# Branch B's v projected 512 columns wide, half of the gate's pieces in attention's opening, and output banks in turn

## The chip, the core and the metric

The kernel runs on one core of a Trainium2 chip. The metric is the device time of one execution in microseconds, from runs of the kernel on the chip; a profiled execution gives the trace that is read here. TensorE (PE) multiplies matrices into PSUM, which has eight banks of 512 float32 columns; VectorE (DVE) and ScalarE (ACT) read PSUM; GpSimd (POOL) works on SBUF alone; the queue of SyncE (SP) issues all DMA transfers, in the order of the program.

## What is computed

One layer on x, 1024 positions of 1024 channels, in float32. It has two parallel attention branches of eight heads each, and everything starts from one modulated, normalised input h:

```
ada = c @ w_ada + b_ada;  shift, scale, gate = split(ada, 3)
h = rms_norm(x, norm_w) * (1 + scale) + shift
cq(384), ckv(256), k_rope(32), gate_a(512), q_b(512), k_b(512), v_b(512), f_b(8),
    gate_b(512), mg_a(1024), mg_b(1024) = split(h @ w_in)
A: latent attention from cq and ckv with rotary parts; B: q_b, k_b normalised, forget-gate bias
y_a = o_a * silu(gate_a);  y_b = o_b * silu(gate_b)
merged = sigmoid(mg_a) * (y_a @ w_branch_a) + sigmoid(mg_b) * (y_b @ w_branch_b)
out = x + gate * (merged @ w_out)
```

The change touches v_b (512 columns of w_in for branch B's v), the `gate` vector of 1024 numbers (c times a third of w_ada, plus a bias) and the last product.

## The kernel before, in words

Every product is made in three matmuls: each operand is split into a rounded high part and the low rest (`split`: ACT copies the high part, DVE subtracts), and hi x hi, hi x lo and lo x hi are summed in one bank. All instructions are issued in the order of the Python program; each engine keeps its own order and waits on semaphores.

The stages. `phase0` makes h, transposed, as hT_hi and hT_lo. `latents`, `g2q` (4 steps) and `g2k` (4 steps, L771) make branch A's q, k and v and store them in DRAM. `attention` (L1239) runs the 16 heads, eight of A and then eight of B, each in 12 steps of scores, softmax, transposes and products. `output` (L1299) makes the last product in 16 units of 24 matmuls.

Between these, a generator of filler work, `fillers` (L909), is advanced by `fill_to` (L142) until a planned TensorE time is reached; a matmul of n columns counts n / 2.4 + 2 ns there. The filler begins with `g1b` (L805), the projection of branch B's q, k and v. It works on six chunks of 256 columns of weights (ci 0 and 1 for q, 2 and 3 for k, 4 and 5 for v). A chunk has four units, each of two blocks of 128 positions in one bank; a unit is 48 matmuls and pauses after every six, which makes eight pieces a unit and 192 pieces in all. The next chunk's weights (two loads of 512 KB) are requested in a chunk's first unit and split in its second and third. A v unit is evacuated by ACT and DVE into `vhl` and stored one unit later (`store_b`, L875). When q, k and v are done, `fillers` goes on with the units named f: the gates, the merge gates and, at the end, the two branches' projections, whose loads of the first weight are started by `hook` from inside g1b.

The accumulators of the filler alternate over the bank tags in `self.fbanks` (`fbank`, L905): "fo" until q, k and v are done, then "fg", and "fgott" after attention. `output` took its banks in its own order, "ttof".

The gate vector is made on DVE: eight pieces, each a load of 512 KB (`gate_load`, L881) and one multiplication with a sum (`gate_sum`, L885). Before, pieces 0 to 3 are summed within g2k's first two steps and 4 to 7 at the beginning of attention; `gate_row` (L894), at head 3, step 0, adds the bias and transposes the column on TensorE (pgT). In attention's opening (L1247 to L1268) the first pair's q and k are loaded (qs, ks) and transposed (qt, kt) in five steps, and then seven score blocks of head 0 follow, each with 1500 ns of filler.

Of the kernel before, what the change touches and what calls it, by code (L numbers as in the profile page):

```python
# [10 lines left out]
F32 = mybir.dt.float32  # L11
F32R = mybir.dt.float32r
# [7 lines left out]
P = 128  # L20
S = 1024
D = 1024
KT = 8
# [51 lines left out]
class Net:  # L75
# [729 lines left out]
    def g1b(self, hook):  # L805
# [4 lines left out]
        def load(ci):  # L810
            if ci < 6:
                w[ci] = [self.load_w(t["w_b"][ci, :, 4 * e:4 * e + 4], [P, 4, 256], f"b{ci}_{e}") for e in range(2)]
# [5 lines left out]
        for ci in range(6):  # L818
            kind, half = ci // 2, ci % 2
            for sp in range(4):  # L820
                if sp == 0:
                    load(ci + 1)
                if sp in (1, 2) and ci < 5:
                    w[ci + 1][sp - 1] = self.split(w[ci + 1][sp - 1], f"b{ci + 1}_{sp - 1}")
                if ci == 5 and sp in (0, 2):
                    hook()
                acc = self.fbank(f"b{ci}_{sp}")
                for i in range(2):
                    st = 2 * sp + i
                    sl = slice(st * P, (st + 1) * P)  # L830
                    for kt in range(KT):
                        wh, wl = w[ci][kt // 4]
                        for e, (a, b) in enumerate(((self.hT_hi, wh), (self.hT_hi, wl), (self.hT_lo, wh))):
                            self.mm(acc[:, i * 256:(i + 1) * 256], a[:, kt, sl], b[:, kt % 4],
                                    kt == 0 and e == 0, kt == KT - 1 and e == 2)
                            if e == 2 and kt % 2 and (i, kt) != (1, KT - 1):
                                yield False
                a3 = acc.rearrange("p (g d) -> p g d", d=64)
                if kind == 2:
                    vhl = U.get([P, 8, P], F32R, f"bv{ci}_{sp}")  # L840
                    nc.scalar.copy(vhl[:, :, 0:64], a3)
                    nc.vector.tensor_tensor(out=vhl[:, :, 64:128], in0=a3, in1=vhl[:, :, 0:64].bitcast(F32), op=ALU.subtract)
                    self.store_b((self.vb_d[2 * sp:2 * sp + 2, :, half * 4:half * 4 + 4].rearrange("s p h d -> p s h d"),
                                  vhl.bitcast(F32).rearrange("p (s h) d -> p s h d", s=2), (U, vhl)))
                else:
                    o = Hs.get([P, 8, 64], F32, f"bo{ci}_{sp}")
                    sq = Hs.get([P, 8, 64], F32, f"bsq{ci}_{sp}")
                    nc.scalar.copy(o, a3)
                    nc.scalar.activation(sq, o, AF.Square)
                    if sp == 0:  # L850
                        ssq = self.sp.tile([P, 32], F32, tag="bssq", bufs=2, name=f"bssq{ci}")
                        outs = []
                    nc.vector.reduce_sum(ssq[:, 8 * sp:8 * sp + 8], sq, axis=AX.X)
                    Hs.put(sq)
                    self.store_b()
                    outs.append(o)
                    if sp == 3:
                        r = self.rsqrt(ssq, 32, 64, f"b{ci}_{sp}")
                        dst = (self.qb_d, self.kb_d)[kind]
                        items = []  # L860
                        for j, o in enumerate(outs):
                            nc.vector.tensor_tensor(out=o, in0=o, op=ALU.mult,
                                                    in1=r[:, 8 * j:8 * j + 8].unsqueeze(2).broadcast_to([P, 8, 64]))
                            items.append((dst[2 * j:2 * j + 2, :, half * 256:half * 256 + 256].rearrange("s p c -> p s c"),
                                          o.rearrange("p (s h) d -> p s (h d)", s=2), (Hs, o)))
                        self.store_b(*items)
                if sp == 3:
                    for pair in w.pop(ci):
                        U.put(*pair)
                if (ci, sp) == (5, 3):  # L870
                    self.store_b()
                    self.g1b_done = True
                yield 1000.0

# [19 lines left out]
    def gate_row(self):  # L894

        nc = self.nc
        nc.vector.tensor_tensor(out=self.gcol, in0=self.gcol, in1=self.b_gate, op=ALU.add)
# [341 lines left out]
    def attention(self):  # L1239
        N = len(self.seq)  # L1240
# [58 lines left out]
    def output(self):  # L1299
# [12 lines left out]
        for u in range(2 * ST):  # L1312
# [21 lines left out]
    def build(self):  # L1334
# [36 lines left out]
        with tc.manual_schedule():  # L1371
            with tc.tile_pool(name="ps2a", bufs=1, space=PSUM) as self.ps2:
# [26 lines left out]
                for sp in range(4):  # L1399
# [3 lines left out]
                    if sp < 3:  # L1403
# [22 lines left out]
def layout(i):  # L1426
# [39 lines left out]
    o["w_b"] = np.stack([_chunks(w_in[:, 1184 + 256 * c:1184 + 256 * (c + 1)], 8) for c in range(6)])  # L1466
# [28 lines left out]
```

## Time and profile before

| | |
|---|---|
| timed runs, median of 3 | 973.12 us (972.27 to 975.09) |
| the profiled execution | 970.98 us |
| its span, first to last instruction | 969.0 us |
| mean granted TensorE clock | 0.998 of 2.4 GHz |
| TensorE busy, share of the span | 98% |
| DVE, ACT, POOL busy | 66%, 49%, 21% |
| filler's q, k, v matmuls (b) | 88.7 to 285.4 us |
| DMA moved | 124.99 MB, mean 129 GB/s |

The busy share of TensorE is that of a pipelined engine: the durations of neighbouring matmuls overlap, so the time that a matmul costs is the distance from one start to the next. Idle time of another engine costs nothing by itself. The granted clock is shown as a share of 2.4 GHz; a row that shows less than 1.00 has a part at 1.2 GHz.

### The profile page before, as it was taken

The page shows a single profiled execution, that of the slowest core. Times are in us where ns is not written, and L with a number is a line of the kernel's source. Part 1 is how long each engine was busy: PE and PEld are TensorE (multiplying, and loading weights), DVE is VectorE, ACT ScalarE, POOL GpSimd, SP SyncE. Part 2 cuts the span into 40 slices and gives each one's busy share as a digit, 9 for nine tenths or more (in the row PEclk, how much of TensorE's full clock was granted, in tenths as well). Part 3 has the DMA queues.
Part 4 walks back from the last instruction along what each step waited for, and adds up shares of the span by engine and source line. Part 5 has one row for each costly group of instructions (what it writes and reads, how often), then busy time and mean ns, then how long its engine had stood idle before and what let it go on. Part 6 is the DMA issues. An engine that isn't in the chain of part 4 may idle for free.

```text
span 969.0 us, 15332 instructions
## 1 busy us (share of the span) xinstructions
PE 952.2 (98%) x5582; PEld 832.3 (86%) x5582; DVE 636.0 (66%) x1379; ACT 477.6 (49%) x959; POOL 204.0 (21%) x260
## 2 busy tenths in 40 slices
PE   7999999999999999999999999999999999999998
PEld 7999999999988888788888888888888878887887
DVE  3967977787646667567667676677676766596222
ACT  7776634443245656546555566465655644143000
POOL 0022132200011222122233233232332220045000
PEclk9999999999999999999999999999999999999999
DMA  9821132864943224225232232322411554633321
GB/s 348 322 95 45 50 116 81 295 225 169 312 134 98 87 67 131 66 74 155 79 109 67 66 90 67 114 85 88 132 56 44 185 185 153 245 141 125 109 88 66
DMA packets 80987, 124.99 MB, mean 129 GB/s; under 512 B 5928, under 2 KB 47536, under 8 KB 80912
## 3 DMA queue, kind: packets, MB, share of 16 engines
q1 hardware_dynamic: 80912, 124.01, 39.3%
q8 instruction: 44, 0.72, 0.3%
q14 instruction: 31, 0.25, 0.1%
HBM read 88.33 MB, written 35.66 MB: 128 GB/s over the span
## 4 chain that ended last, share of the span: by engine, by line
PE 89%; DVE 4%; DMA 3%; ACT 2%; issue 2%; POOL 0%; SPq 0%; ACTq 0%; DVEq 0%
PE f L127 31%; PE b L127 12%; PE out L127 9%; PE s L127 9%; PE o L127 7%; PE pt L136 6%; PE q L127 3%; PE ckv L127 2%; PE kv L127 2%; PE cq_s L127 2%; DVE hT_lo L998 1%; DMA ks_u<-ka_d 1%; PE cq_t L127 1%; DVE mg_h L991 1%; PE pada L127 1%
## 5 line engine op out<-in xcount | busy, mean ns | idle before, releaser
L1192 ACT CAST pp_u<-pt 128x512 fp32r<-128x512 f32 x192 | 92.2, 480 | 178.9 <-PE pt L136 164.9
L1193 DVE TENSOR_TENSOR pp_u<-pt,pp_u 128x512 fp32r<-128x512 f32 x192 | 106.5, 555 | 76.5 <-ACT pp_u L1192 74.4
L127 PE MATMUL f<-hT_hi,hi_f_u 128*128 128x512 f32 x384 | 153.9, 401 | 0.0
L127 PE MATMUL f<-hT_lo,hi_f_u 128*128 128x512 f32 x384 | 153.7, 400 | 0.0
L127 PE MATMUL f<-hT_hi,lo_f_u 128*128 128x512 f32 x384 | 153.5, 400 | 0.0
L127 PE MATMUL s<-k_u,q_u 96*128 96x512 f32 (+6 forms) x480 | 117.1, 363 | 1.2 <-ACT p_h L1172 0.7
L127 PE MATMUL b<-hi_b_u,hT_hi 128*128 128x256 f32 x384 | 109.6, 286 | 0.0
L127 PE MATMUL b<-hi_b_u,hT_lo 128*128 128x256 f32 x384 | 108.6, 283 | 0.0
L127 PE MATMUL b<-lo_b_u,hT_hi 128*128 128x256 f32 x384 | 108.6, 283 | 0.0
L1176 POOL TENSOR_SCALAR p_u<-p_u,rs 128x640 f32<-128x640 f32 (+1 forms) x64 | 64.7, 1011 | 169.1 <-DVE rs L1175 93.2
L1166 DVE TENSOR_REDUCE nm<-s 128x1 f32<-128x128 f32 (+7 forms) x128 | 97.0, 758 | 4.4
L127 PE MATMUL o<-pp_u,v_u 128*128 128x512 f32 (+7 forms) x384 | 94.4, 340 | 0.0
L1176 POOL TENSOR_SCALAR p_h<-p_h,rs 128x128 f32<-128x128 f32 (+1 forms) x64 | 36.9, 577 | 249.3 <-DVE rs L1175 220.0
L127 PEld LDWEIGHTS s<-k_u,q_u 96*128 96x128 f32 (+2 forms) x480 | 77.1, 191 | 7.0 <-ACT p_h L1172 1.2
L127 PEld LDWEIGHTS f<-hT_hi,lo_f_u 128*128 128x128 f32 x384 | 72.5, 189 | 12.0
L127 PEld LDWEIGHTS f<-hT_hi,hi_f_u 128*128 128x128 f32 x384 | 72.7, 189 | 11.1
L127 PEld LDWEIGHTS f<-hT_lo,hi_f_u 128*128 128x128 f32 x384 | 72.5, 189 | 11.2
L127 PEld LDWEIGHTS o<-pp_u,v_u 128*128 128x128 f32 (+1 forms) x384 | 62.0, 162 | 19.7 <-issue 0.2
L127 PEld LDWEIGHTS b<-lo_b_u,hT_hi 128*128 128x128 f32 x384 | 73.6, 192 | 0.3
L127 PEld LDWEIGHTS b<-hi_b_u,hT_hi 128*128 128x128 f32 x384 | 73.6, 192 | 0.3
L127 PEld LDWEIGHTS b<-hi_b_u,hT_lo 128*128 128x128 f32 x384 | 73.6, 192 | 0.0
L136 PEld LDWEIGHTS pt<-ident,p_u 128*128 128x128 f32 x416 | 52.7, 140 | 16.7
(310 smaller groups left out, 1998.5 us busy)
## 6 DMA issues: line engine op xcount, KB each, us to landing
raw_f_u<-in_w_t SPq DMA_DIRECT2D x24, 512.0 KB
wada_u<-in_w_ada SPq DMA_DIRECT2D x16, 512.0 KB
mg_d<-th_h SPq DMA_DIRECT2D x32, 256.0 KB
mg_h<-mg_d SPq DMA_DIRECT2D x32, 256.0 KB
raw_b_u<-in_w_b SPq DMA_DIRECT2D x12, 512.0 KB
x_u<-in_x SPq DMA_DIRECT2D x8, 512.0 KB
raw_wg_u<-in_w_gate SPq DMA_DIRECT2D x8, 512.0 KB
va_d<-vhl_u SPq DMA_DIRECT2D x8, 512.0 KB
```

The costliest lines, as they stand in the source:

```text
L127: self.nc.tensor.matmul(out, lhsT=l, rhs=r, start=start, stop=stop)
L136: self.nc.tensor.transpose(out=out, in_=in_, identity=self.ident)
L991: nc.vector.scalar_tensor_tensor(out=m, in0=m, scalar=1.0, in1=acc, op0=ALU.add, op1=ALU.mult)
L998: nc.vector.tensor_tensor(out=self.hT_lo[x], in0=mA[c1][:, x[2]], in1=self.hT_hi[x].bitcast(F32), op=ALU.subtract)
L1166: nc.vector.tensor_reduce(out=nm, in_=sv, axis=AX.X, op=ALU.max, negate=True)
L1176: nc.gpsimd.tensor_scalar(out=p[:, 0:w], in0=p[:, 0:w], scalar1=rs, scalar2=0.0, op0=ALU.mult, op1=ALU.add)
L1192: nc.scalar.copy(ph[:, c0:], pt[:, c0:])
L1193: nc.vector.tensor_tensor(out=pl[:, c0:], in0=pt[:, c0:], in1=ph[:, c0:].bitcast(F32), op=ALU.subtract)
```

## The change

1. g1b's chunks 4 and 5 become one v part. Its weights come as four loads of two of the eight row blocks each, all 512 columns wide (bv_0 to bv_3), requested in k's last chunk (ci 3). They are split in that chunk: bv_0 and bv_1 in its second and third unit, as before for a next chunk, bv_2 at the start of its fourth unit, and bv_3 in the middle of that unit, when the first half of chunk 3's weights has been given back. v then has eight units of 24 matmuls of 512 columns, one block of 128 positions each, with a pause after every three. `hook` is called before the second and the sixth of them; before, it was called before units 1 and 3 of chunk 5.
2. Gate pieces 4 to 7 are no longer loaded in g2k but in the opening of attention: 4 and 5 after the third of its five first steps, 6 and 7 after the fifth, where 4 and 5 are summed; 6 and 7 are summed before the sixth score block, where the bias is added too. It was added in `gate_row` before.
3. `output` takes its accumulators from `fbank`, in turn over "fgott".

```diff
--- before.py
+++ after.py
@@ -808,22 +808,22 @@
         def load(ci):
-            if ci < 6:
+            if ci == 4:
+                w[4] = [self.load_w(t["w_bv"][:, 2 * e:2 * e + 2], [P, 2, 512], f"bv_{e}") for e in range(4)]
+            elif ci < 4:
                 w[ci] = [self.load_w(t["w_b"][ci, :, 4 * e:4 * e + 4], [P, 4, 256], f"b{ci}_{e}") for e in range(2)]
...
-        for ci in range(6):
+        for ci in range(4):
             kind, half = ci // 2, ci % 2
             for sp in range(4):
                 if sp == 0:
                     load(ci + 1)
-                if sp in (1, 2) and ci < 5:
+                if sp in (1, 2) or (ci, sp) == (3, 3):
                     w[ci + 1][sp - 1] = self.split(w[ci + 1][sp - 1], f"b{ci + 1}_{sp - 1}")
-                if ci == 5 and sp in (0, 2):
-                    hook()
@@ -833,44 +833,60 @@
...
                             self.mm(acc[:, i * 256:(i + 1) * 256], a[:, kt, sl], b[:, kt % 4],
                                     kt == 0 and e == 0, kt == KT - 1 and e == 2)
+                            if (ci, sp, i, kt, e) == (3, 3, 1, 3, 2):
+                                U.put(*w[3][0])
+                                w[4][3] = self.split(w[4][3], "b4_3")
                             if e == 2 and kt % 2 and (i, kt) != (1, KT - 1):
                                 yield False
...
-                if kind == 2:
-                    vhl = U.get([P, 8, P], F32R, f"bv{ci}_{sp}")
-                    nc.scalar.copy(vhl[:, :, 0:64], a3)
-                    nc.vector.tensor_tensor(out=vhl[:, :, 64:128], in0=a3, in1=vhl[:, :, 0:64].bitcast(F32), op=ALU.subtract)
-                    self.store_b((self.vb_d[2 * sp:2 * sp + 2, :, half * 4:half * 4 + 4].rearrange("s p h d -> p s h d"),
-                                  vhl.bitcast(F32).rearrange("p (s h) d -> p s h d", s=2), (U, vhl)))
-                else:
...
+                if sp == 3:
+                    for pair in w.pop(ci)[ci // 3:]:
                         U.put(*pair)
-                if (ci, sp) == (5, 3):
-                    self.store_b()
-                    self.g1b_done = True
                 yield 1000.0
+        w = w[4]
+        for st in range(ST):
+            if st in (1, 5):
+                hook()
+            acc = self.fbank(f"bv_{st}")
+            sl = slice(st * P, (st + 1) * P)
+            for kt in range(KT):
+                wh, wl = w[kt // 2]
+                for e, (a, b) in enumerate(((self.hT_hi, wh), (self.hT_hi, wl), (self.hT_lo, wh))):
+                    self.mm(acc, a[:, kt, sl], b[:, kt % 2], kt == 0 and e == 0, kt == KT - 1 and e == 2)
+                if st == ST - 1 and kt % 2:
+                    U.put(*w[kt // 2])
+                if kt < KT - 1:
+                    yield False
+            a3 = acc.rearrange("p (g d) -> p g d", d=64)
+            vhl = U.get([P, 8, P], F32R, f"bvhl_{st}")
+            nc.scalar.copy(vhl[:, :, 0:64], a3)
+            nc.vector.tensor_tensor(out=vhl[:, :, 64:128], in0=a3, in1=vhl[:, :, 0:64].bitcast(F32), op=ALU.subtract)
+            self.store_b((self.vb_d[st], vhl.bitcast(F32), (U, vhl)))
+            if st == ST - 1:
+                self.store_b()
+                self.g1b_done = True
+            yield 1000.0
@@ -894,7 +910,6 @@
-        nc.vector.tensor_tensor(out=self.gcol, in0=self.gcol, in1=self.b_gate, op=ALU.add)
         pg = self.bank("t", "pgT")
@@ -1247,14 +1262,21 @@
         next(preps[0])
         self.fill_to(self.pe_time + 10000)
         self.load_v(0)
-        self.gate_sum(range(4, 8))
-        self.U.put(self.cb)
-        for _ in range(5):
+        for i in range(5):
             next(preps[0])
             self.fill_to(self.pe_time + 1500)
+            if i == 2:
+                self.gate_load((4, 5))
+            if i == 4:
+                self.gate_sum((4, 5))
+                self.gate_load((6, 7))
         for c, i in enumerate((0, 4, 1, 5, 2, 3, 6)):
             if c == 3:
                 self.load_v(1)
+            if c == 5:
+                self.gate_sum((6, 7))
+                self.U.put(self.cb)
+                nc.vector.tensor_tensor(out=self.gcol, in0=self.gcol, in1=self.b_gate, op=ALU.add)
@@ -1321,7 +1343,7 @@
-                acc = self.bank("ttof"[(u + e) % 4], f"out{u}{e}")[:, ls]
+                acc = self.fbank(f"out{u}{e}")[:, ls]
@@ -1400,7 +1422,7 @@
                     self.g2k(sp)
                     if sp < 2:
                         self.gate_sum((2 * sp, 2 * sp + 1))
-                    if sp < 3:
+                    if sp < 1:
                         self.gate_load((2 * sp + 2, 2 * sp + 3))
                     self.fill_to(self.pe_time + 6500)
@@ -1463,7 +1485,8 @@
-    o["w_b"] = np.stack([_chunks(w_in[:, 1184 + 256 * c:1184 + 256 * (c + 1)], 8) for c in range(6)])
+    o["w_b"] = np.stack([_chunks(w_in[:, 1184 + 256 * c:1184 + 256 * (c + 1)], 8) for c in range(4)])
+    o["w_bv"] = _chunks(w_in[:, 2208:2720], 8)
```

The rest of the diff moves q's and k's evacuation, which is unchanged, one level to the left.

## Rows read from the trace of the kernel before

**Rows 1.** Page, parts 1, 2 (GB/s in 40 slices of 24.2 us) and 5.
```profile
PE 952.2 (98%) x5582; PEld 832.3 (86%) x5582; DVE 636.0 (66%) x1379; ACT 477.6 (49%) x959; POOL 204.0 (21%) x260
...
GB/s 348 322 95 45 50 116 81 295 225 169 312 134 98 87 67 131 66 74 155 79 109 67 66 90 67 114 85 88 132 56 44 185 185 153 245 141 125 109 88 66
...
L127 PE MATMUL b<-hi_b_u,hT_hi 128*128 128x256 f32 x384 | 109.6, 286 | 0.0
```

**Rows 2.** Waits of TensorE, whole span: who <- for whom: us, times, longest.
```profile
PE pgT L136 <- DVE gcol L897: 2.4, 1, 2.4
PE out L127 <- DVE mg_h L991: 1.7, 1, 1.7
PE kt L136 <- DMA ks_u<-ka_d: 1.6, 1, 1.6
PE s L127 <- ACT p_h L1172: 0.7, 1, 0.7
```

**Rows 3.** Chain of waits, pieces in order of time: start us, us, what.
```profile
217.56 2.75 PE kv L127 x12
...
225.92 7.19 PE b L127 x60
...
258.81 10.16 DMA ks_u<-ka_d
...
815.76 16.66 PE f L127 x73
```

**Rows 4.** Timeline around pgT, DVE and PE: start us, us, instruction [idle before <-releaser].
```profile
391.07 0.29 DVE L1193 TENSOR_TENSOR pp_u<-pt,pp_u 128x128 fp32r<-128x128 f32 x1
...
393.83 0.16 DVE L1175 RECIPROCAL rs<-sm 128x1 f32<-128x1 f32 x1 [0.64 <-ACT p_u L1172]
393.91 0.15 DVE L897 TENSOR_TENSOR gcol<-gcol,vec 128x8 f32<-128x8 f32 x1
394.11 0.27 PE L136 MATMUL pgT<-ident,gcol 128*8 128x128 f32 x1 [2.40 <-DVE gcol L897]
```

**Rows 5.** Windows after pgT: us, busy PE PEld DVE ACT POOL, granted clock, DMA, GB/s.
```profile
394.10:395.30 1.20, 1.19 (x6) 1.01 (x7) 0.28 (x1) 0.00 (x0) 1.03 (x1) 1.00 0.00 0
...
395.30:398.80 3.50, 3.50 (x13) 2.76 (x12) 0.68 (x1) 1.64 (x3) 0.00 (x0) 0.53 0.83 202
```

**Rows 6.** Timeline, PE and DVE, from the last f to the first output.
```profile
875.54 0.39 PE L127 MATMUL f<-yhi_u,lo_f_u 128*128 128x512 f32 x1
...
876.87 0.68 DVE L991 SCALAR_TENSOR_TENSOR mg_h<-mg_h,f 128x512 f32<-128x512 f32 x1
...
877.60 0.50 PE L127 MATMUL out<-hi_wo_u,hT_hi 128*128 128x512 f32 x1 [1.68 <-DVE mg_h L991]
...
880.12 1.46 DVE L998 TENSOR_TENSOR hT_lo<-mA_u,hT_hi 128x512 fp32r<-128x512 f32 x2
```

**Rows 7.** Timeline in g2k, DVE and the SP queue.
```profile
231.45 1.29 DVE L800 TENSOR_TENSOR kraw_h<-kraw_h,y_g2k 128x512 f32<-128x512 f32 x2
...
236.63 2.16 SPq L877 DMA_DIRECT2D kb_d<-bo_h  x4
```

**Rows 8.** Tiles raw_b_u and raw_wg_u: count, ns min/median/max, first and last start.
```profile
L116 DVE TENSOR_TENSOR lo_b_u<-raw_b_u,hi_b_u x24: 675/682/1224, 85.7 to 249.4; 128x512 fp32r<-128x512 f32 x24
...
L890 DVE SCALAR_TENSOR_TENSOR raw_wg_u<-raw_wg_u,cb_u x8: 1212/1219/1221, 204.3 to 261.3; 128x1024 f32<-128x1024 f32 x8
```

**Rows 9.** Timeline of attention's opening, SP, PE and DVE.
```profile
259.58 4.34 SPq L1047 DMA_DIRECT2D k_u<-kr_d  x4
...
269.11 0.63 PE L136 MATMUL kt<-ident,ks_u 128*128 128x128 f32 x4 [1.58 <-DMA ks_u<-ka_d]
...
274.31 0.45 PE L127 MATMUL s<-k_u,q_u 96*128 96x128 f32 x3
...
289.71 0.11 DVE L1164 MEMSET s<- 64x64 f32 x1 [1.87 <-PE s L127]
...
294.64 0.33 PE L136 MATMUL pt<-ident,p_h 128*128 128x128 f32 x1 [0.32 <-POOL p_h L1176]
```

**Rows 10.** Waits of the SP queue, 183 to 300 us: us, times, longest.
```profile
SPq L877 <- DVE bv_u L842: 17.9, 5, 8.3
```

More of the change, by code (lines that the diff above doesn't have):

```diff
@@ L838, in g1b @@
                 a3 = acc.rearrange("p (g d) -> p g d", d=64)
-                if kind == 2:
-                    vhl = U.get([P, 8, P], F32R, f"bv{ci}_{sp}")
-                    nc.scalar.copy(vhl[:, :, 0:64], a3)
-                    nc.vector.tensor_tensor(out=vhl[:, :, 64:128], in0=a3, in1=vhl[:, :, 0:64].bitcast(F32), op=ALU.subtract)
-                    self.store_b((self.vb_d[2 * sp:2 * sp + 2, :, half * 4:half * 4 + 4].rearrange("s p h d -> p s h d"),
-                                  vhl.bitcast(F32).rearrange("p (s h) d -> p s h d", s=2), (U, vhl)))
-                else:
[L846 to L854, printed above, removed]
-                    self.store_b()
[L856 to L866, printed above, removed]
@@ L867, in g1b @@
-                if sp == 3:
-                    for pair in w.pop(ci):
+                o = Hs.get([P, 8, 64], F32, f"bo{ci}_{sp}")
+                sq = Hs.get([P, 8, 64], F32, f"bsq{ci}_{sp}")
+                nc.scalar.copy(o, a3)
+                nc.scalar.activation(sq, o, AF.Square)
+                if sp == 0:
+                    ssq = self.sp.tile([P, 32], F32, tag="bssq", bufs=2, name=f"bssq{ci}")
+                    outs = []
+                nc.vector.reduce_sum(ssq[:, 8 * sp:8 * sp + 8], sq, axis=AX.X)
@@ new lines, in g1b @@
+                Hs.put(sq)
+                self.store_b()
+                outs.append(o)
+                if sp == 3:
+                    r = self.rsqrt(ssq, 32, 64, f"b{ci}_{sp}")
+                    dst = (self.qb_d, self.kb_d)[kind]
+                    items = []
+                    for j, o in enumerate(outs):
+                        nc.vector.tensor_tensor(out=o, in0=o, op=ALU.mult,
+                                                in1=r[:, 8 * j:8 * j + 8].unsqueeze(2).broadcast_to([P, 8, 64]))
+                        items.append((dst[2 * j:2 * j + 2, :, half * 256:half * 256 + 256].rearrange("s p c -> p s c"),
+                                      o.rearrange("p (s h) d -> p s (h d)", s=2), (Hs, o)))
+                    self.store_b(*items)
@@ L869, in g1b @@
+                if sp == 3:
+                    for pair in w.pop(ci)[ci // 3:]:
                         U.put(*pair)
-                if (ci, sp) == (5, 3):
-                    self.store_b()
-                    self.g1b_done = True
                 yield 1000.0
+        w = w[4]
[18 more added lines that the diff above has]
+            if st == ST - 1:
+                self.store_b()
+                self.g1b_done = True
+            yield 1000.0
@@ L1239, in attention @@
     def attention(self):
-        N = len(self.seq)
+        nc, N = self.nc, len(self.seq)
         preps = {n: self.prep_a(n) if n < 8 else self.prep_b(n) for n in range(0, N, 2)}
```

## Prediction

> **What bounds the kernel now.** I read the engine shares first: TensorE is busy 952.2 of 969.0 us, DVE two thirds and ACT half [rows 1]. So a microsecond comes from fewer or shorter matmuls, or from a place where TensorE stands. Second, TensorE's waits over the whole span: besides the start there are four of note, pgT 2.4, out 1.7, kt 1.6 and s 0.7 us [rows 2], and the change touches the code at all four. Third, the chain of waits for the spacing of the matmuls, because a matmul's own duration (286 ns in the groups [rows 1]) overlaps its neighbours'. Last, timelines around each wait, to see what is late next. The reader should see that hardly any cover is left: whatever delays TensorE is added to the end. The profiled execution took 970.98 us (969.0 of span, 2.0 around it); I make the sum against it, and add 2.1 at the end, because the median of the timed runs is 973.12.
>
> **v at 512 columns.** Branch B has 3 x 384 matmuls of 256 columns in six weight chunks [rows 1]; v has two of the six, so 384. They become 192 of 512. Spacing: 60 matmuls of 256 in 7.19 us are 119.8 ns; 73 of 512 in 16.66 us are 228.2 ns; 12 of kv in 2.75 us, just after the narrow ones, 229.2 ns [rows 3]. So 46.0 us become 43.8: **-2.2 us** (-2.0 by kv's rows). The reason is a fixed part of about 11 ns in each matmul (2 x 119.8 - 228.2), paid half as often. The evacuations stay eight of 128x512 on ACT and DVE, the eight stores stay 512 KB each.
>
> The Trainium skill speaks against this term: its page TensorE: Matmul & The Clock Gate, section "Wait — 56ns, not 53.3ns?", gives a warm matmul's spacing as columns over 2.4 GHz plus about 2.5 ns. By that, as an estimate, 109.2 and 215.8 ns, the term would be -0.5 us and the whole change -5.1. The rows above do not agree with so small a fixed part.
>
> **The gate bias, added early.** At (3, 0) TensorE reaches pgT and stands 2.40 us, because the addition to gcol is queued on DVE behind a reciprocal that itself waits 0.64 us for ACT's sum [rows 4]. The change makes the addition in the opening, over 100 us earlier. pgT then needs its "t" bank alone, whose last reader starts at 391.07 and takes 0.29 us [rows 4], before TensorE stops at 391.7. There is more: the granted clock was 0.53 over the 3.5 us from 395.3 on, against 1.00 just before [rows 5]: nearly all of it at 1.2 GHz instead of 2.4. That cost 0.47 x 3.5 = 1.65 us of work, and the only idle stretch ahead of it is this one. Both go: **-4.1 us**. At worst something else holds TensorE as long: 0.
>
> **Output banks in turn.** The first output takes the "t" bank that the last unit but one of branch B's projection filled, and DVE is behind there: TensorE waits 1.68 us for its mg_h (876.87, 0.68 us) [rows 6]. In turn over five banks it takes the bank filled four units earlier, long free. Next is the last operand: hT_lo's final two pieces start at 880.12, 1.46 us for both [rows 6], so the first, which the first output needs in its last matmul, is there at about 880.8. From 875.77 that matmul, 23 spacings of 228 ns later, comes at 881.0. A tie: **-1.7 us**, at worst 0.
>
> **v's weights split early.** In the order of issue k's last chunk ends in piece 128 of 192 (a piece is six narrow matmuls or three wide ones, 652 and 646 ns in the planner's account), three pieces into the fill after the third g2k. Two v splits move from v's units into k's last unit. The last is issued behind that g2k's own DVE work, which ends with two products from 231.45, 1.29 us [rows 7]. A split's two differences take 0.68 us each [rows 8], 0.6 apart like those two products, so its first half is ready at about 233.4. The first v unit starts at 225.92 + 18 x 0.12 = 228.1 [rows 3] and wants that half in its 20th matmul, 19 x 0.228 later, at 232.4. TensorE stands: **+1.0 us** (0 to 1.6). On ACT the split's copies lie ahead of one evacuation, which has the idle TensorE time after it. The split it replaces, two units later, hid behind narrow matmuls, so nothing is earned there. Its 1.3 us on DVE also delay the normalised k, for whose store the SP queue waits until 236.63 [rows 7], and behind that store stand all stores and loads of attention's opening.
>
> **The opening: loads.** ks lands 10.16 us after its issue [rows 3], and the first kt transposes wait 1.58 us for it [rows 9]. Ahead of it lie the same bytes as before (the first f weight load now ahead of the stores instead of among them), so it lands about 1 us later (1.3 from the queue's start, less what the earlier f load fills). TensorE gets there 1.0 later by the stall above, 0.5 earlier by the shorter pieces (48 of 0.685 against 46 of 0.72). **+0.3 us** (-1.6 if ks is in time, +1.0).
>
> Four of eight gate loads move here. The first two (1.05 MB) are put between ks and the four loads of k's rotary rows, and behind a v store that waits for its evacuation. At 312 GB/s of this stretch [rows 1] they are 3.4 us on the queue. Before, those four issues began at 259.58 and the scores that read them started at 274.31 [rows 9]; no view names their landing. If they trail ks by one store and two gate loads, some 5 us, they meet the scores, which are also 5 us behind ks (274.31 - 269.11). I take **0**, with 0 to +3; a price below 0 is excluded, for a later issue cannot help.
>
> **The opening: DVE.** A gate piece is 1.22 us [rows 8]. Four stood ahead of q's products, where TensorE did not wait. Now two stand ahead of the first row maximum: the scores need that bank again only two steps later, some 5 us, so nothing. Two more and the bias stand ahead of the maximum of (0, 3). DVE is idle 1.87 us just before it [rows 9] and the sums take 2.4; the transposes after it already wait 0.32 us for POOL [rows 9], so **+0.6 us** (0 to 2.4). The s wait of 0.7 [rows 2] came from the last v evacuation on DVE between two score steps; that is now one step earlier: **-0.7** (0 at worst).
>
> Hooks and store order shift nothing else on TensorE: f's count and its order of banks stay, four of its matmuls just begin a step earlier.
>
> **Sum.** -2.2 - 4.1 - 1.7 + 1.0 + 0.3 + 0 + 0.6 - 0.7 = -6.8, so 964.2 for a profiled execution, and 966.3 for the median of timed runs.
>
> **Rivals** (all on the timed scale).
> 1. The opening gets worse: ks or k's rotary rows land so late that TensorE stands 2 to 3 us more and, as after pgT's 2.40, falls to 1.2 GHz for 1.65. For it: 1.6 us are late already, and the queue starts later. Against it: waits of 1.58 and 1.68 us left the clock at 1.00. -6.8 + 2.5 + 1.65 = -2.7: 970.4. Chance 0.18.
> 2. pgT's wait is only handed on: the reciprocal and ACT's sum are as late as before, and the next transposes or scores wait for them, with the clock drop. For it: TensorE arrives 2.4 us earlier at everything after. Against it: the next scores come some 3 us of f matmuls later, and the other even heads show no wait at this place [rows 2]. -6.8 + 4.1 = -2.7: 970.4. Chance 0.10.
> 3. The wide matmuls gain nothing, by a smaller fixed part than the rows show, or by v pieces that alternate with transposes: -6.8 + 2.2: 968.5. Chance 0.07. The page above would make nearly this.
> 4. All gains and no new wait, ks in time: -2.2 - 4.1 - 1.7 - 0.7 - 1.6 = -10.3: 962.8. Chance 0.15.
> 5. Slower: the SP queue, in order, stands at a v store for as long as it did once before, 8.3 us [rows 10], now with two gate loads and k's rotary rows behind it instead of ahead. The scores then wait about 8.3, plus 1.65 at 1.2 GHz: -6.8 + 10 = +3.2: 976.3. It decides from the point where those rows land more than 7 us after the scores are due. Against it: the store they now follow is of a unit that ends in TensorE's order well ahead. Chance 0.04.
>
> **Numbers.** The forecast, 964 to 968.5, has 0.46. The predicted time is 966.3. The range 962.0 to 970.6 leaves out rival 5 and the tails of 1, 2 and 4. A measurement of this kernel tells about 0.3%, 2.9 us, from no change: faster is below 970.2. The forecast, rivals 3 and 4 and some four tenths of 1 and 2 make faster 0.79; most of the rest of 1 and 2 makes the same 0.16; slower 0.05.
>
> **What would show it.** In the changed kernel's rows: b at 256 columns 768 and v 192 matmuls of 512 at 227 to 232 ns; no wait at pgT and no stretch below 1.00 at 395 us; the first out directly behind the last f; a wait of about 1 us in the first v unit on lo_b; kt waiting about 2 us. A wait of over 2 us in 228 to 295 us with a clock below 1.00 would make the prediction wrong upward; a kt that does not wait, downward.

## The result, and the profile after

The changed kernel takes 962.75 us (median of four runs, 961.75 to 964.47) against 973.12 for the kernel before, run beside it: ratio 0.9892, 95% interval 0.9865 to 0.9918, so 1.1% faster. A fourth execution of the kernel before, at 1172.23 us, was in the slow state and is not counted. Forecast were 966.3 and a range of 962.0 to 970.6, with "faster" as the likeliest. The profiled execution took 961.75 us, span 959.9 (before: 970.98 and 969.0).

Page of the changed kernel, part 1 (before: [rows 1]):

```profile
PE 947.9 (99%) x5390; PEld 820.6 (85%) x5390; DVE 633.2 (66%) x1379; ACT 477.3 (50%) x959; POOL 208.1 (22%) x260
```

TensorE's waits over the whole span (who, for whom: us, times, longest), to be laid beside [rows 2]:

```profile
PE warm L136 <- DMA ident<-in_ident: 4.6, 1, 4.6
PE xt L136 <- DVE x_u L286: 1.0, 1, 1.0
PE bv L127 <- DVE lo_b_u L116: 1.0, 1, 1.0
PE s L127 <- DMA k_u<-kr_d: 0.9, 2, 0.6
PE pt L136 <- POOL p_h L1191: 0.3, 1, 0.3
```

All four waits of before are gone, pgT, out, kt and s, and two small new ones have come: bv at 233 us for a low half of its weights, and s in attention's opening for k's rotary rows. The wait of xt lies in phase0; the first b starts at 88.70 us as before (88.72). Around pgT, where TensorE stood 2.40 us [rows 4], it now runs through, and the 3.5 us behind it have the full clock (0.53 in [rows 5]). Timeline of TensorE, then the window (us, busy PE PEld DVE ACT POOL, granted clock, DMA, GB/s):

```profile
389.83 0.60 PE L136 MATMUL pt<-ident,p_h 128*128 128x128 f32 x4
390.27 0.27 PE L136 MATMUL pgT<-ident,gcol 128*8 128x128 f32 x1
390.29 0.48 PE L127 MATMUL f<-hT_hi,lo_f_u 128*128 128x512 f32 x1
```

```profile
391.50:395.00 3.50, 3.50 (x19) 2.86 (x18) 2.10 (x7) 2.22 (x5) 1.01 (x1) 1.00 0.33 92
```

The first output starts one spacing, 0.23 us, behind the last f ([rows 6] had 1.68 us of idle time there):

```profile
868.45 0.39 PE L127 MATMUL f<-yhi_u,lo_f_u 128*128 128x512 f32 x1
868.68 0.39 PE L127 MATMUL out<-hi_wo_u,hT_hi 128*128 128x512 f32 x1
```

v's spacing, from the chain: twelve wide matmuls take the same 2.72 us as the twelve of kv ahead of them, 226.7 ns each.

```profile
234.80 2.72 PE kv L127 x12
237.52 2.72 PE bv L127 x12
```

The new bv wait, in the timeline of DVE and TensorE, and the first store behind it on the SP queue ([rows 7]: 236.63):

```profile
231.42 1.29 DVE L800 TENSOR_TENSOR kraw_h<-kraw_h,y_g2k 128x512 f32<-128x512 f32 x2
232.63 1.29 DVE L116 TENSOR_TENSOR lo_b_u<-raw_bv_u,hi_b_u 128x512 fp32r<-128x512 f32 x2
233.37 0.50 PE L127 MATMUL bv<-lo_b_u,hT_hi 128*128 128x512 f32 x1 [1.00 <-DVE lo_b_u L116]
237.81 2.17 SPq L893 DMA_DIRECT2D kb_d<-bo_h  x4
```

The reader sees the split queued directly behind g2k's two products, and TensorE starting as its first half ends. The opening, SP queue and TensorE ([rows 9]):

```profile
258.38 0.38 SPq L1054 DMA_DIRECT2D ks_u<-ka_d  x1
265.51 0.33 SPq L893 DMA_DIRECT2D vb_d<-bvhl_u  x1
265.95 1.23 SPq L102 DMA_DIRECT2D raw_wg_u<-in_w_gate  x2
267.24 1.88 SPq L1062 DMA_DIRECT2D k_u<-kr_d  x4
```

```profile
268.25 0.60 PE L136 MATMUL kt<-ident,ks_u 128*128 128x128 f32 x4
273.98 0.30 PE L127 MATMUL s<-k_u,q_u 96*128 96x128 f32 x1 [0.55 <-DMA k_u<-kr_d]
274.62 0.41 PE L127 MATMUL s<-k_u,q_u 96*128 96x128 f32 x2 [0.35 <-DMA k_u<-kr_d]
```

kt starts without a wait: ks landed (the last update of its semaphore in the trace) at 267.97 in place of 268.97, and TensorE came to kt at 268.25 in place of 267.53. Behind ks the SP queue stands for 6.8 us until a v unit is evacuated, and only then issues the gate loads and k's rotary rows, which come 0.9 us late for the scores.

To compare traces I take, from the first b matmul to the start of the last out, TensorE's idle time and half of the time at 1.2 GHz out of the stretch; what is left is its matmuls at full clock ("rest"):

| us | idle | half clock | rest |
|---|---|---|---|
| before | 7.67 | 1.71 | 866.88 |
| after | 2.67 | 0 | 864.54 |

That is -5.00 - 1.71 - 2.34 = -9.05, the whole difference of the spans.

### The profile page after: what moved, and what is told of

Same layout as the page of the kernel before. It is cut to its first block, busy times and chain, and to the rows that moved or that the text cites. A ratio compares the mean times of both kernels' runs of the same rounds, so it can differ in the third digit from the quotient of the medians.

```text
span 959.9 us, 14942 instructions
## 1 busy us (share of the span) xinstructions
PE 947.9 (99%) x5390; PEld 820.6 (85%) x5390; DVE 633.2 (66%) x1379; ACT 477.3 (50%) x959; POOL 208.1 (22%) x260
## 4 chain that ended last, share of the span: by engine, by line
PE 92%; DMA 3%; DVE 2%; ACT 2%; issue 1%; SPq 1%; POOL 0%; ACTq 0%; DVEq 0%; POOLq 0%
PE f L127 36%; PE out L127 9%; PE s L127 9%; PE b L127 8%; PE o L127 7%; PE pt L136 6%; PE q L127 3%; PE ckv L127 2%; PE kv L127 2%; PE cq_s L127 2%; PE bv L127 1%; PE cq_t L127 1%; DMA x_u<-in_x 1%; PE pada L127 1%; DMA va_d<-vhl_u 1%
## 5 line engine op out<-in xcount | busy, mean ns | idle before, releaser
L1191 POOL TENSOR_SCALAR p_h<-p_h,rs 128x128 f32<-128x128 f32 (+1 forms) x64 | 41.7, 652 | 247.3 <-DVE rs L1190 208.2
L127 PE MATMUL b<-hi_b_u,hT_hi 128*128 128x256 f32 x256 | 73.1, 285 | 0.0
L127 PE MATMUL b<-hi_b_u,hT_lo 128*128 128x256 f32 x256 | 72.4, 283 | 0.0
L127 PE MATMUL b<-lo_b_u,hT_hi 128*128 128x256 f32 x256 | 72.4, 283 | 0.0
L136 PE MATMUL pt<-ident,p_u 128*128 128x128 f32 x416 | 66.2, 272 | 0.0
L1187 ACT ACTIVATE p_u<-s,nm 128x640 f32<-128x640 f32 (+1 forms) x64 | 61.5, 961 | 4.3 <-DVE nm L1181 3.2
L127 PE MATMUL out<-lo_wo_u,hT_hi 128*128 128x512 f32 (+1 forms) x136 | 51.2, 377 | 0.0
```

The source lines that it names most:

```text
L127: self.nc.tensor.matmul(out, lhsT=l, rhs=r, start=start, stop=stop)
L136: self.nc.tensor.transpose(out=out, in_=in_, identity=self.ident)
L1187: nc.scalar.activation(p[:, 0:w], sv, AF.Exp, bias=nm, accum_out=sm)
L1191: nc.gpsimd.tensor_scalar(out=p[:, 0:w], in0=p[:, 0:w], scalar1=rs, scalar2=0.0, op0=ALU.mult, op1=ALU.add)
```

## The experiments

Each is timed against the kernel before; several share its runs. The runs also list their mean granted clock, and it explains most of the spread. The kernel before, 65 runs: 1.000 in 4 of them (median 969.0 us), 0.998 in 19 (971.8), 0.996 in 20 (974.4), 0.994 or 0.995 in 19 (976.0), and 0.997 or 0.999 in the other three. A stretch of some 3.4 us at 1.2 GHz, as in [rows 5], takes 0.0018 off that mean, so by these clocks an execution has none to three of them; the profiled one of before had one. The mean also takes in the end of the span, where TensorE has nothing left to do. In the changed kernel's trace the clock is low there and nowhere else, so a mean of 0.999 need not hold a slow stretch:

```profile
958.20:959.90 1.70, 0.00 (x0) 0.00 (x0) 0.00 (x0) 0.00 (x0) 0.00 (x0) 0.50 0.11 35
```

### The bias early, alone

```diff
+        self.nc.vector.tensor_tensor(out=self.gcol, in0=self.gcol, in1=self.b_gate, op=ALU.add)  # behind gate_sum(range(4, 8))
     def gate_row(self):
-        nc.vector.tensor_tensor(out=self.gcol, in0=self.gcol, in1=self.b_gate, op=ALU.add)
```

> The kernel before, with one edit: the gate's bias is added in attention's opening, right behind the sums of pieces 4 to 7. My theory: TensorE's idle time of 2.40 us at pgT was DVE's late addition, and the 3.5 us at half clock behind it (1.65 us of work) came from that idle time alone, so both go: the profiled span falls from 969.0 to 964.9 us, no wait at pgT, no stretch below 1.00 near 395 us. Rival, the wait is handed on: ACT's sum and the reciprocal are as late, the next transposes or scores wait for them: span 969.0. Rival, the half clock has another cause: only 2.40 go, span 966.6, and the granted clock still falls near 393 to 399 us.

Measured: 968.75 us, ratio 0.995 (0.9929 to 0.9972); span 965.4. No wait at pgT and nothing in its place nearby, so the wait was not handed on. TensorE's waits:

```profile
PE kt L136 <- DMA ks_u<-ka_d: 2.4, 1, 2.4
PE out L127 <- DVE mg_h L990: 1.3, 1, 1.3
```

The span came 0.5 us over the expected one, mostly by kt, which waited 2.42 in this execution. And here is the first thing I had not expected: behind that idle time, as long as pgT's, the clock stayed whole.

```profile
270.50:274.00 3.50, 3.50 (x32) 3.50 (x32) 2.11 (x3) 3.41 (x6) 0.00 (x0) 1.00 0.07 23
```

### Output banks in turn, alone

```diff
-                acc = self.bank("ttof"[(u + e) % 4], f"out{u}{e}")[:, ls]
+                acc = self.fbank(f"out{u}{e}")[:, ls]
```

> The kernel before, with one edit: output takes its banks in turn over 'fgott', as the merge before it did. My theory: the 1.68 us that TensorE stood ahead of the first output was the wait for the bank that DVE had not yet read, so the first output starts right behind the last f: span 969.0 - 1.7 = 967.3 us. Rival, the wait is handed on to the last operand (the first of hT_lo's final two pieces, which the first output needs in its last matmul): TensorE stands as long, later in that unit: 969.0. Between them I called it a tie: a remaining wait of a few tenths on hT_lo, span 967.3 to 967.7.

Measured: 972.0 us, ratio 0.998 (0.9957 to 1.0003), span 967.3. The first out starts one spacing behind the last f, without a wait on hT_lo: the term is right, by the trace; the timed runs alone do not tell this kernel from the one before. And the span fits by luck. pgT's wait of 2.40 is still there, and this time no half clock followed; two waits near 785 us (o 0.76, s 1.24 in place of 0.49) took 1.5 us back. The window behind pgT:

```profile
395.20:398.70 3.50, 3.50 (x19) 2.83 (x19) 1.53 (x4) 1.66 (x3) 0.00 (x0) 1.00 0.84 214
```

### v narrow again, in the changed kernel

```diff
-        for ci in range(4):          # k's last chunk, then v in eight units of 512 columns
+        for ci in range(6):          # g1b and w_b as before; hook() in units (4, 1) and (5, 1)
```

> The changed kernel with v made as before, in two chunks of 256 columns (384 matmuls in place of 192), its branch projections' first loads started at the same share of v as in the changed kernel; gate pieces, bias and output banks stay changed. Span of the changed kernel 959.9 us. My theory, a fixed part of about 12 ns in each matmul: 384 x 119.8 = 46.0 against 192 x 226.7 = 43.5 us, +2.5, less the wait of 1.0 us for bv_3's split, which the narrow form did not have: 961.4. Rival, by a fixed part of 2.5 ns: +0.5 - 1.0, so 959.4, faster than the changed kernel. Third: v's width is also what moved the opening (the waits for xt, k's rows), then the sum of the waits in 250 to 295 us differs from the changed kernel's 0.9 + 0.3.

Measured: 965.24 us, ratio 0.9917 (0.9885 to 0.9949), span 965.3, 3.9 over the first theory's, for the waits and the half clock named below and a wait of 0.8 on p_u. The rest is 866.24, 1.70 over the changed kernel's. Over all traces of this study it is 866.24 to 867.15 with narrow v (five kernels, mean 866.74) and 864.13 to 864.61 with wide v (eight; mean 864.39; a ninth, whose slow stretch lies for over 1 us inside a wait, is left out): -2.35 us, against -2.2 forecast; the single pair of traces scatters by 0.6 around it. That is far from the -0.5 of the rival. The third theory holds as well: kt waits 2.22 us again, with half clock behind it, and s 0.7 on ACT's p_h.

```profile
PE kt L136 <- DMA ks_u<-ka_d: 2.2, 1, 2.2
PE s L127 <- ACT p_h L1171: 0.7, 1, 0.7
```

That last wait is in all five kernels with narrow v and gone in eight of nine with wide v, which fits the reason I had given for it (v's evacuation, one step earlier).

### Gate pieces back in g2k

```diff
+        self.gate_sum(range(4, 8))   # and cb given back, bias added: right behind load_v(0)
-            if i == 2: self.gate_load((4, 5))
-            if i == 4: self.gate_sum((4, 5)); self.gate_load((6, 7))
-            if c == 5: self.gate_sum((6, 7)) ...
-                    if sp < 1:
+                    if sp < 3:
                         self.gate_load((2 * sp + 2, 2 * sp + 3))
```

> The changed kernel with gate pieces 4 to 7 loaded and summed where the kernel before does it (loads in g2k's second and third step, sums at the beginning of attention, the bias right behind them); wide v and output banks stay changed. It undoes the move of half of the gate's pieces alone. My theory: the move bought nothing and cost the scores' wait for k's rows, so the span is 959.9 - 0.9 = 959.0, ks with nothing directly behind it lands 1.6 us behind the store ahead of it and kt does not wait. Rival: the four pieces in the opening relieved DVE and the SP queue in g2k; put back, 1 to 2 us of waits come up in 200 to 262 us: 961 to 962. Rival: four sums (4.9 us) ahead of q's products now delay qt or kt, which they did not before: 961.

Measured: 961.02 us, ratio 0.9892 (0.9863 to 0.9921), span 959.1, as the theory said to 0.1 us. Moving half of the gate's pieces bought nothing; it cost the wait for k's rows. All that the change gained by the gate is the bias.

### k's rotary rows one step later, in the kernel before

```diff
-                for j, x in enumerate(ops[nm, e]): ...dma_start(x[64:96], ...)   # k, pair 0: with ks's first group
+        for e in range(0 if n else 2): rows("k", e, 0)                           # ... with its second
         group("k", src, self.vka, 1)
```

> The kernel before, with one edit: head pair 0's four loads of k's rotary rows are issued one step later, so behind the next v store, and not directly behind ks. It asks why ks was in time in the changed kernel. First theory (my forecast's): ks's landing is set by the bytes ahead of it. Then nothing changes: ks lands at about 269.0, some 2.3 to 2.9 us behind the store ahead of it, and kt waits 1.1 to 2.4 us as in the three kernels with this order. Second theory: what is issued directly behind ks shares its DMA engines and delays its last part; with nothing directly behind it, ks lands 1.6 us behind the store ahead of it, as in the changed kernel: at about 267.7, and kt waits 0.2 to 0.7 us. The rows themselves still land by 272, ahead of the scores at 273 to 274.

Measured: the SP queue now has the store between ks and the rows, and kt does not wait at all. Timelines of SP and TensorE:

```profile
258.70 0.38 SPq L1039 DMA_DIRECT2D ks_u<-ka_d  x1
264.60 0.36 SPq L877 DMA_DIRECT2D vb_d<-bv_u  x1
265.01 2.47 SPq L1051 DMA_DIRECT2D k_u<-kr_d  x4
```

```profile
267.33 0.63 PE L136 MATMUL kt<-ident,ks_u 128*128 128x128 f32 x4
```

ks landed at 267.20, 1.63 us behind the store ahead of it. That is the second theory, 0.5 us better than it said. The time did not show it (972.09 us, ratio 0.9993, 0.9972 to 1.0014; span 969.6), because this execution had half clock twice, from the end of pgT's wait (2.39) on and behind out, whose wait was 1.86:

```profile
392.10:395.50 3.40, 3.18 (x9) 2.40 (x10) 0.45 (x3) 0.60 (x1) 1.01 (x1) 0.50 0.43 114
876.80:880.20 3.40, 3.40 (x9) 2.62 (x9) 3.29 (x6) 1.58 (x3) 0.00 (x0) 0.50 0.13 49
```

### The rows directly behind ks, in the changed kernel

```diff
         src = load("k", self.ka_d)
+        if n == 0: operands("k")     # the four loads of the rows
         yield
-        operands("k")
+        if n: operands("k")
```

> The changed kernel with one edit, the reverse of the one before: head pair 0's four loads of k's rotary rows are issued directly behind ks, ahead of the v store. First theory (bytes ahead of ks alone): ks lands at 268.0 as before, kt does not wait, and the scores' wait of 0.9 us goes because the rows are there by 270: span 959.0. Second theory (what follows directly delays it): ks lands 2.3 to 2.9 us behind the store ahead of it in place of 1.62, at 268.6 to 269.3, and kt waits 0.4 to 1.1 us, which takes the place of the scores' 0.9: span about 959.5 to 960.

Measured: 960.84 us, ratio 0.9875 (0.984 to 0.991), span 958.8. ks landed at 268.20, 3.33 us behind the store ahead of it, and kt waits 0.4, as the second theory said; the scores' 0.9 are gone. The evidence is weaker than in the run before: the store ahead landed 1.5 us earlier than in the changed kernel (264.87, there 266.35), so in time from the span's start ks came hardly later than the 268.0 of the first theory, and only its distance from that store grew.

```profile
PE kt L136 <- DMA ks_u<-ka_d: 0.4, 1, 0.4
```

All traces together, by what the SP queue issues behind ks: with rows or gate loads within 1.3 us (before and five others) ks lands 2.27 to 3.73 us behind the store ahead of it; with nothing for five us or more 1.62 to 1.65 in seven of eight. The eighth is the last run below, at 3.72. It differs from the seven in one thing: its next transfer was issued 1.53 us before the first of ks's semaphore updates, in the seven at most 0.71 before it. In 264 to 266 us its DMA engines had no pause, as in the six with transfers close behind (share 1.06 to 1.18); in six of the seven they had one (0.45 to 0.67; the other 1.04). So what is queued behind may count by when ks is served, not by when it is issued; one trace does not show it. The window in the changed kernel, then in the last run:

```profile
264.00:266.00 2.00, 2.00 (x12) 1.66 (x11) 1.96 (x3) 1.99 (x4) 0.00 (x0) 1.00 0.45 121
264.00:266.00 2.00, 2.00 (x11) 1.64 (x10) 2.00 (x4) 1.05 (x2) 0.00 (x0) 1.00 1.12 308
```

### Gate pieces 4 and 5 behind the rows

```diff
-            if i == 2:
+            if i == 3:
                 self.gate_load((4, 5))
```

> The changed kernel with one edit: gate pieces 4 and 5 are loaded behind k's rotary rows (after the fourth of the five opening steps) and not ahead of them. My theory: the 0.55 + 0.35 us that the first scores wait for k's rows are the two gate loads (1 MB) ahead of them on the SP queue. So the rows land some 3 us earlier (last one at about 272.5 in place of 275.70), the wait goes, and the median falls by 0.9 and by what clock loss goes with it: span 959.0 at an unbroken clock. The sums of 4 and 5 then wait on DVE for their data until about 276, which delays the first row maximum by 1 to 2 us; TensorE needs that bank again only at 279.95, so 0. Rival: that delay reaches TensorE (a wait at the second or third score block of 1 to 2 us): 960 to 961. Rival: the rows were late because the DMA engines were busy, not because of their place: they land as before and the wait of 0.9 stays.

Measured: 960.78 us (960.19 to 961.16, six runs), ratio 0.987 (0.9847 to 0.9894), span 958.4. The order on the SP queue and the scores, now without a wait:

```profile
258.05 0.38 SPq L1054 DMA_DIRECT2D ks_u<-ka_d  x1
265.18 0.33 SPq L893 DMA_DIRECT2D vb_d<-bvhl_u  x1
265.61 2.15 SPq L1062 DMA_DIRECT2D k_u<-kr_d  x4
267.86 1.79 SPq L102 DMA_DIRECT2D raw_wg_u<-in_w_gate  x4
```

```profile
272.95 0.45 PE L127 MATMUL s<-k_u,q_u 96*128 96x128 f32 x3
```

The rows landed by 271.37 in place of 275.70: their place on the queue was the cause. The granted clock was 0.999 or 1.000 in all six runs.

### The same, and the sums of 4 and 5 later

```diff
+            if c == 3:
+                self.gate_sum((4, 5))     # not in the last of the five steps
```

> The changed kernel with gate pieces 4 and 5 loaded behind k's rotary rows, as in the other run of this set, and also summed later: not in the last opening step but ahead of the fourth score block, where DVE stood idle for 2.47 us. My theory: the scores' 0.9 us go as in the other run and DVE's queue is not held by late gate data, so span 959.0, with no new wait in 274 to 290 us. Rival: the sums (2 x 1.2 us) delay the maximum of the fourth block and TensorE waits 0.5 to 1 us at the sixth: 959.5 to 960. If the other run shows a DVE that is not in the way, both come out the same.

Measured: 961.18 us, ratio 0.9874 (0.9851 to 0.9898), span 958.8, no new wait: the same as the run before, so DVE was not in the way there.

### The bias late again, with the rows in time

```diff
     def gate_row(self):
+        nc.vector.tensor_tensor(out=self.gcol, in0=self.gcol, in1=self.b_gate, op=ALU.add)   # and not at c == 5
```

> The changed kernel with gate pieces 4 and 5 behind k's rotary rows and with the gate's bias put back to head 3, where it was before: so one long wait, pgT's, in a kernel that has no other above 1.0 us. My theory: the wait of 2.4 us comes back whole (span 958.4 + 2.4 = 960.8 at an unbroken clock). What I had costed as certain, 1.65 us of half clock behind it, is open: it followed this wait in two of the three traces that have it and not in the third. If it follows as often, the mean of (1 - granted clock) x span over the runs rises by about 1 us from 0.2, single runs lie at 962.8 or at 964.5, and the median is 3 to 4 us above 960.78. Rival, the half clock has nothing to do with this wait: it stays at 0.2, all runs near 962.8. Rival, it follows every time: all near 964.5.

Measured: 964.09 us (962.90 to 966.20), ratio 0.9919 (0.9898 to 0.994). That is 3.3 over 960.78, within the 3 to 4 expected (the two sets ran on different chips; by the ratios it is 4.8). The wait came back with 2.13 us; the mean of (1 - clock) x span rose from 0.16 to 1.28 us. That rise says less than I had expected of it, for the listed clocks go in steps of 0.001, which is 0.96 us, and take in the end of the span: a whole slow stretch makes 0.998, and two of the six runs show that, four 0.999. In the profiled execution the half clock followed:

```profile
392.20:395.70 3.50, 3.50 (x12) 2.61 (x11) 0.27 (x1) 1.10 (x2) 0.43 (x1) 0.51 0.73 179
```

So the wait costs its length, and some 1.7 us more in a part of the executions: three runs near 963 (962.90 to 963.43) and three from 964.75 up are neither all near 962.8 nor all near 964.5, and both rivals fall.

### bv_3's differences on POOL

```diff
-                                w[4][3] = self.split(w[4][3], "b4_3")
+                                w[4][3] = self.split(w[4][3], "b4_3", engine=nc.gpsimd)
```

> The changed kernel with one edit: the differences of bv_3's split are made by POOL, which does nothing between 220 and 245 us, in place of DVE, whose work on g2k lies ahead of them. My theory: the 1.00 us that TensorE stands in the first v unit is DVE's queue alone, so it goes: POOL's difference of 128x512 took 1.59 us (in the 16 such pieces of w_out's split), ACT's copy of the first half is there at about 228.9, so the low half at 230.5, and TensorE wants it at 232.4. Span 959.9 - 1.0 = 958.9 us; the store of k then also starts about 1.3 us earlier (236.6 instead of 237.8). Rival, the second half is late instead (ready 232.1 or, if POOL is slowed by DVE beside it, after 233.1): a wait of a few tenths is left, 959.2 to 959.6. Rival, an earlier queue brings k's rotary rows or ks into collision and the opening gives it back: 959.9.

Measured: 963.73 us, ratio 0.9899 (0.9869 to 0.9929), span 962.5. The bv wait is gone, yet k's store starts at 238.93, later than before, not earlier: while POOL ran, two tiny instructions of DVE took 1.19 and 1.22 us, where the same two took 0.17 each in the changed kernel. POOL and DVE:

```profile
229.24 2.55 POOL L116 TENSOR_TENSOR lo_b_u<-raw_bv_u,hi_b_u 128x512 fp32r<-128x512 f32 x2 [42.97 <-ACT hi_b_u L115]
```

```profile
229.39 1.19 DVE L88 TENSOR_SCALAR v_g2k<-kssq 128x16 f32<-128x16 f32 x1
230.61 1.22 DVE L89 TENSOR_SCALAR y_g2k<-v_g2k 128x16 int32<-128x16 int32 x1
231.86 0.18 DVE L93 SCALAR_TENSOR_TENSOR a_g2k<-y_g2k 128x16 f32<-128x16 f32 x1
```

The Trainium skill, page SBUF — State Buffer, section "SBUF: two separate sides", says that DVE in some modes and GpSimd lock a shared pair of ports for a whole instruction, and the loser is fully blocked. The rows agree: the two end at 230.57 and 231.83, POOL's differences at 230.54 and 231.79. k's rows then landed as late as 276.77 (275.70 in the changed kernel) and the scores waited 1.75 and 0.58, with half clock behind them:

```profile
PE s L127 <- DMA k_u<-kr_d: 2.3, 2, 1.7
```

So the loss is at the place of the third case I had named. That the late store of k brought it is not shown: ks and the v store behind it landed 0.4 to 0.5 us earlier than in the changed kernel (267.52 and 268.86), and only the gate loads and the rows came later. Part of the wait is TensorE's own earlier coming, by the bv wait that is gone. In the three runs at a clock of 1.000 the spans are 959.8 to 961.0, so the 1.0 us of the first theory did not come in any.

### The kv step two pieces earlier

```diff
-                    self.fill_to(self.pe_time + 6500)
+                    self.fill_to(self.pe_time + (5200 if sp == 2 else 6500))   # gate pieces 4, 5 behind the rows
```

> The changed kernel with two edits: gate pieces 4 and 5 behind k's rotary rows (that run had a span of 958.4 us and left one wait of 1.00 us, for bv_3's low half), and the fill behind the third g2k step shortened by two pieces (6500 to 5200 ns of planned time), so that the 12 kv matmuls of the fourth step, 2.75 us, come ahead of the two v pieces that need bv_3. My theory: the low half is late by DVE's queue and fixed at about 233.4 us, so 2.7 us of other work ahead of its reader cover the wait of 1.00 in full: span 957.4, median 1 us under that run's 960.78. Rival: kv's evacuation then competes with the split on DVE and ACT, and the wait moves to the last kv or to the next g2k operand: 958.4. Rival: the stores of k and v, one step earlier, collide again with ks or the rows (kt or scores wait 0.3 to 1): 957.7 to 958.4.

Measured: 968.46 us, ratio 0.9954 (0.9938 to 0.997), span 965.7: a clear miss. The bv wait is gone as meant, but two pieces fewer lay ahead of the opening: the next v store was not yet due, so the rows stood directly behind ks again (258.30 and 259.58), ks landed 2.72 us behind the store ahead of it, and TensorE was at kt two us earlier. Half clock followed that wait (269.11 to 272.52).

```profile
PE kt L136 <- DMA ks_u<-ka_d: 3.0, 1, 3.0
PE s L127 <- ACT p_u L1187: 1.2, 1, 1.2
PE s L127 <- ACT p_h L1187: 1.1, 2, 0.7
```

### The same, with the two pieces given back

```diff
+                    self.fill_to(self.pe_time + (6500, 6500, 5200, 7800)[sp])
```

> As the run with the earlier kv step, but the two pieces are given back to the fill behind the fourth g2k step (5200 and then 7800 ns of planned time), so that everything from attention's opening on stands in the same order as in the run with gate pieces behind k's rows (span 958.4, median 960.78). The wait of 1.00 us for bv_3 goes by the 2.75 us of kv ahead of its reader. First theory: that wait costs its full 1.00, as I costed it: span 957.4. Second theory: the opening is timed by the DMA queue, whose start (the store of k) does not depend on that wait; there ks landed at 267.50 and kt began at 267.91, so TensorE coming 1.0 us earlier waits 0.6 for ks: span 958.0. Third: the order of stores shifts again, with the v store behind the rows: kt waits 2 us or more, 960 to 962.

Measured: 959.86 us, ratio 0.9853 (0.9827 to 0.9879), the fastest median of the study, though not told apart from 960.78. Five of six runs have spans of 957.5 to 958.5 at a clock of 1.000; their median, 957.9, is 1.1 under the 959.0 of the six runs without this edit. That fits a bv wait worth its full 1.00 (first theory), but the two sets ran on different chips, and no trace of the five shows where the time went. The sixth, the profiled one, has no bv wait either, yet 963.7: ks landed 3.72 us behind the store ahead of it, kt waited 3.31, and 6.8 us at half clock began in that wait, at 269.23. Why ks was late in this execution stays open.

```profile
PE kt L136 <- DMA ks_u<-ka_d: 3.3, 1, 3.3
```

## Why the prediction was right, and by which steps

- **v at 512 columns**: -2.2 forecast, -2.34 in the pair of traces, -2.35 over 13. Right, by the fixed part of a matmul, which the prediction's rows had at 11 ns and these at 13 (2 x 119.8 - 226.7). The Trainium skill has about 2.5 ns (page TensorE: Matmul & The Clock Gate, section "Wait — 56ns, not 53.3ns?"); no run here agrees with it, and the measurement decides.
- **The bias early**: -4.1 forecast, -2.40 - 1.71 in the pair. Right for these two executions, but its second half was not a certainty. Half clock followed pgT's wait in three of the four traces that have it.
- **Output banks**: -1.7, measured -1.67; the tie with hT_lo went to TensorE.
- **bv_3's split**: +1.0, measured 1.00, at the matmul and by the queue named. The medians of the last run fit a cost that reached the end.
- **ks**: +0.3 forecast, -1.58 measured. The step that failed is "it lands about 1 us later": ks landed 1.00 us earlier, and TensorE came 0.7 later. I counted the bytes ahead of ks and the start of the queue, and not what is issued behind it. Moving k's rows alone took kt's wait away in the kernel before (1.58 to 0, ks 1.8 us earlier) and brought 0.4 into the changed one. How a transfer behind delays the one ahead, and why the last run's ks was late all the same, stays open.
- **k's rotary rows**: 0 forecast, with 0 to +3; measured +0.9, by the two gate loads ahead of them, at the place named.
- **Gate sums 6, 7 and the bias**: +0.6 forecast, 0 measured: pt waits 0.3 as before.
- **The s wait**: -0.7, measured -0.75. A second one, 0.5 us on p_u near 786, went too; I had no term for it. It is there in all five kernels with narrow v (0.5 to 1.2 us) and in one wide; why is not shown.

The sum: -9.05 against -6.8, and ks makes most of the difference (-1.9), against the rows' +0.9. On the timed scale the gap is larger, -10.4 against the forecast's -6.8, because I added 2.1 us to go from the profiled execution to the median, as if that were a constant. By the granted clocks of the 65 runs it was mostly slow stretches: one in the profiled execution of before, and one or two in its median. The changed kernel has fewer waits that could bring one, and its median stands only 1.0 over its profile. Rival 4, 962.8, meets the number but not the mechanism: it had no bv wait and no wait for the rows. Rivals 1, 2, 3 and 5 did not come true. Of the prediction's own signs all came but one: kt does not wait, which it had named as the sign of being wrong downward. The time lies below the band of the forecast itself, 964 to 968.5, and 0.75 us inside the range. So v's width, the bias, the banks and bv_3's split are right by their mechanism. ks was wrong by 1.9 us, the rows by 0.9, the gate sums by 0.6, and 1.1 of the 2.1 us between profile and median were not there; that the whole stayed in the range with these is in part luck.

## What to carry to other kernels

A wait on TensorE that nothing covers costs its length, and now and then a slow stretch on top: cost the first as certain and the second as a chance, and read the granted clocks of many runs, not of one profile. When a transfer is needed soon, look at what is issued directly behind it on the queue as well as at what is ahead; here its place moved ks by 1.8 us. What is needed last goes last. When an edit removes a small wait, look which stores and loads change places behind it: here 1.00 us removed brought 3 us of another wait, and with the order restored one execution in six still had it.

## What the runs showed of the hardware that I had not expected

The length of an idle stretch alone does not tell whether the clock falls behind it. It fell to 1.2 GHz in or behind 3.31 and 3.04 (the two runs with the kv step earlier, kt), 2.40 (before, pgT), 2.39 and 1.86 (rows late), 2.22 (narrow v, kt), 2.13 (bias late) and 1.75 us (POOL, s, with 0.58 more close behind); it stayed at 2.4 GHz behind 2.42 (bias early, kt), 2.40 (banks in turn, pgT) and 1.68 and 1.58 (before). What decides is not settled by these runs.

With transfers issued close behind it, ks landed 0.6 to 2.1 us later behind the store ahead of it (2.27 to 3.73 against 1.62 to 1.65), though it was issued first. The Trainium skill, page DMA: Bandwidth & Descriptors, section "Two DMAs through the same engine are not ordered", says that within one queue of a DMA engine descriptors start in order but are pipelined. The traces agree that transfers overlap: with the rows directly behind ks in the changed kernel, the first update of their semaphores came at 264.77 and the last of ks's only at 268.20. The 3.72 us of the last run, with nothing issued behind ks for 6 us, are not explained.
